# Value products of a head pair issued as one block, transposed probabilities written back into their own tiles

## The chip, the cores and the metric

The kernel runs on one core of one Trainium2 chip. The metric is the device time of one execution in microseconds (us); less is better. Five engines share the work: TensorE (PE, with its weight loads shown apart as PEld), VectorE (DVE), ScalarE (ACT), GpSimd (POOL) and SyncE (SP, which here issues the transfers). Everything is computed in 32-bit floats.

## The reference

The reference is a stack of four residual layers over 512 tokens of width 1024: a short convolution (layer A), a sparse attention with an indexer (layer B), a latent attention (layer C) and the convolution once more. The change touches B and C alone. Both end in the same attention over 16 heads of 64 value columns, swept over blocks of 128 queries:

```
logits = jnp.einsum("bqhd,bshd->bhqs", q_b, k) * scale
logits = jnp.where(mask, logits, -jnp.inf)       # key chunk <= query chunk (B: and among its top 128 keys)
p = jax.nn.softmax(logits, axis=-1)
o = jnp.einsum("bhqs,bshd->bqhd", p, v)
...
x = x + (o * jax.nn.silu(z)) @ w_out
```

In layer B `p` is taken over the selected keys only, which the kernel does with an additive mask. A query block t (0 to 3) sees t+1 key blocks of 128, so a head has 1+2+3+4 = 10 pairs of a query block and a key block.

## The kernel before, in words

Both layers call `attention(jobs, filler)` with eight jobs, one for each pair of heads. A job is cut into six chunks: for the query blocks [0, 1], then [2], then [3], one chunk for either head (e = 0, 1). A chunk passes through four steps.

- `scores(c)` (line 607) makes the logits of both heads' chunks c and c+1 on TensorE into the two PSUM banks of tag "s" (L283 in layer B, L1049 in layer C). DVE adds the mask and finds the extremum (L622) while it moves them to two SBUF tiles of tag "p"; ACT takes the exponential and the sum (L625).
- `normalise(c)` multiplies by the reciprocal of the sum (L635 on DVE), on POOL for e = 0 (L640), on ACT for e = 1 (L642).
- `turn(c)` (line 645) transposes the 128x128 blocks of the chunk on TensorE into a PSUM bank of tag "pt" (L651) and copies that bank to SBUF into a tile of tag "pt", on DVE for the last chunk of a job (L655), else on ACT (L657).
- `mix(c)` (line 660) runs behind each odd chunk: for both heads, the values of a key block (128x64) are the stationary operand and the transposed block moves past (L672). Head 0 writes partitions 0 to 63 of the bank of tag "o", head 1 partitions 64 to 127, so these matmuls use half of the array's columns each. Behind the last chunk of the job DVE takes the bank out, times the gate (L677) or as it is (L679, the last two pairs).

The profile counts two matmul instructions for one of these products: a job has 20 products and 40 instructions of line 672.

A loop over c starts `scores` four chunks ahead, then runs `normalise`, `turn(c)`, `mix(c-1)` and the filler: the projections of later groups of heads and the gates (L274 to L276, which add three matmuls each), up to a cost that is set for each chunk. Before the first chunk of a group its projections are completed.

The order on each engine is not quite that of the program. The framework simulates a timeline when the kernel is built, and issues on each engine the earliest instruction in program order whose inputs are ready in that timeline. On the chip each engine then follows the order so fixed.

Tiles come from pools by tag: 6 of tag "p", 4 of tag "pt" in SBUF, and in PSUM 2 banks of tag "pt", 1 of "o", 1 of "tr", 2 of "pj" and the two of "s". A tile can be taken when the last reader of its former content is done. After the attention, `branch_out` splits the eight gated results for the output projection (L714, L715; "po" in the profile), whose first group of columns needs the banks "pt", "pt", "o", "tr".

Of the kernel before, what the change touches and what calls it, by code (L numbers as in the profile page):

```python
# [13 lines left out]
AF = mybir.ActivationFunctionType  # L14
OP = mybir.AluOpType
AX = mybir.AxisListType

P = 128
S = 512
D = 1024  # L20
NK = D // P
NT = S // P
# [47 lines left out]
def encoder(ctx: ExitStack, tc: tile.TileContext, a, out, depth=4):  # L70
# [4 lines left out]
    act_e, dve, pool, pe = nc.scalar, nc.vector, nc.gpsimd, nc.tensor  # L75

    def const(shape, name, dtype=F32):
        return sb.tile(shape, dtype, name=name, bufs=1)


    BUFS = {"gt": 2, "rp": 5, "T": 18, "v": 4, "gate": 10, "p": 6, "pt": 4, "qk": 4, "xh": NK, "xl": NK,
            "raw": 3, "whi": 4, "wlo": 4}
    BANKS = {"pj": 2, "pt": 2, "o": 1, "tr": 1}

    def tile_of(tag, name, shape=(P, S), dtype=F32):
        return sb.tile(list(shape), dtype, name=name, tag=tag, bufs=BUFS[tag])

# [3 lines left out]
    def tiny(name, n, dtype=F32, tag="tiny"):  # L91
        return sb.tile([P, n], dtype, name=name, tag=tag, bufs=24)

    def bank(name, tag):
        return ps.tile([P, S], F32, name=name, tag=tag, bufs=BANKS[tag])

    def two_banks(name):

        b = ps.tile([P, 2, S], F32, name=name, tag="s", bufs=1)
        return [b[:, 0], b[:, 1]]  # L100
# [7 lines left out]
    clock = [0.0]  # L108
# [99 lines left out]
    o = 0  # L208
# [5 lines left out]
    o = 0  # L214
# [64 lines left out]
    def side_by_side(outs, ls, rs):  # L279

        for i, (x, y) in enumerate(((0, 0), (0, 1), (1, 0))):
            for o, l, r in zip(outs, ls, rs):
                nc.tensor.matmul(o, l[x], r[y], start=i == 0, stop=i == 2)  # L283
        clock[0] += 0.00125 * max(256, outs[0].shape[1])
# [302 lines left out]
    def attention(jobs, filler):  # L587

        early_turns[0] = False
        chunks = []
        for j in jobs:
            mine = [(j, e, ts) for ts in ([0, 1], [2], [3]) for e in range(2)]
            for i, c in enumerate(mine):
                chunks.append(c + (j["fill"][0] + (j["fill"][1] - j["fill"][0]) * (i + 1) / len(mine),))
        stage, soft, wide, outs, factors = {}, {}, {}, {}, {}

        def parts(ts):  # L600

            o = 0
            for t in ts:
                yield t, slice(o, o + (t + 1) * P)
                o += (t + 1) * P

        def scores(c):

            j, _, ts = chunks[c][:3]
            if ts[0] == 0:  # L610
                filler.through(j["after"])
            banks = two_banks("s")
            n = len(ts)
            for t, w in parts(ts):
                j["scores"]([b[:, w] for b in banks], t)
            ps_ = [tile_of("p", "p") for _ in range(2)]
            mn = [tiny("mn", n, tag="small") for _ in range(2)]
            sm = tiny("sum", 2 * n, tag="small")
            for e in range(2):
                p = ps_[e]  # L620
                for i, (t, w) in enumerate(parts(ts)):
                    dve.tensor_tensor_reduce(out=p[:, w], in0=banks[e][:, w], in1=j["masks"](t), scale=j["qs"](e, t),  # L622
                                             scalar=-GONE, op0=OP.add, op1=OP.min, accum_out=mn[e][:, i:i + 1])
                for i, (t, w) in enumerate(parts(ts)):
                    act_e.activation(p[:, w], p[:, w], AF.Exp, bias=mn[e][:, i:i + 1], scale=-1.0,  # L625
                                     accum_out=sm[:, e * n + i:e * n + i + 1])
                stage[c + e] = p, sm

        def normalise(c):

            e, ts = chunks[c][1:3]
            p, sm = stage.pop(c)
            if e == 0:
                rc = tiny("rc", 2 * len(ts), tag="small")
                dve.reciprocal(rc, sm)  # L635
                factors[c] = factors[c + 1] = rc
            rc = factors.pop(c)[:, e * len(ts):(e + 1) * len(ts)]
            for i, (t, w) in enumerate(parts(ts)):
                if e == 0:
                    pool.tensor_scalar(p[:, w], p[:, w], rc[:, i:i + 1], None, op0=OP.mult)  # L640
                else:
                    act_e.activation(p[:, w], p[:, w], AF.Copy, scale=rc[:, i:i + 1])  # L642
            soft[c] = p

        def turn(c):
            j, e, ts = chunks[c][:3]
            p = soft.pop(c)
            b = bank("pt", "pt")
            n = sum(t + 1 for t in ts) * P
            for i in range(0, n, P):  # L650
                pe.transpose(b[:, i:i + P], p[:, i:i + P], ident)  # L651
                clock[0] += 0.11
            x = tile_of("pt", "pt")
            if c % 6 == 5:
                dve.tensor_copy(x[:, :n], b[:, :n])  # L655
            else:
                act_e.activation(x[:, :n], b[:, :n], AF.Copy)  # L657
            wide[c] = x

        def mix(c):  # L660
            j, e, ts = chunks[c][:3]
            if e == 0:
                return
            if ts[0] == 0:
                outs[id(j)] = bank("o", "o")
            o = outs[id(j)]
            x = [wide.pop(c - 1), wide.pop(c)]
            for t, w in parts(ts):
                for kb in range(t + 1):
                    i = w.start + kb * P  # L670
                    for e in range(2):
                        pe.matmul(o[64 * e:64 * e + 64, t * P:(t + 1) * P], j["v"](e, kb), x[e][:, i:i + P],  # L672
                                  start=t == 0, stop=t == NT - 1 and kb == t)
                        clock[0] += 0.134
            if ts[-1] == NT - 1:
                if j["gate"]:
                    dve.tensor_tensor(j["dst"](), o, j["dst"](), op=OP.mult)  # L677
                else:
                    dve.tensor_copy(j["dst"](), o)  # L679

        N = len(chunks)
        ahead = 4
        for c in range(-ahead, N + 1):
            if c + ahead < N and c % 2 == 0:
                scores(c + ahead)
            if 0 <= c + ahead - 1 < N:
                normalise(c + ahead - 1)
            if 0 <= c < N:
                turn(c)
            if c > 0:  # L690
                mix(c - 1)
            if c + ahead < N:
                filler.to(chunks[c + ahead][3])
        while filler.step():
            pass
        early_turns[0] = True
# [23 lines left out]
    def layer_b(last):  # L720
# [42 lines left out]
        def select():  # L763
            for t in range(1, NT):
                n = (t + 1) * P
                sc = None
                for pair in range(4):
                    banks = two_banks("si")
                    ws = [slice(0, 64), slice(64, 128)]
                    side_by_side([b[:, :n] for b in banks], [[x[w, t * P:(t + 1) * P] for x in iT[pair]] for w in ws],  # L770
                                 [[x[w, :n] for x in kiT] for w in ws])
                    for e, b in enumerate(banks):
                        rel = tile_of("p", "rel")
                        act_e.activation(rel[:, :n], b[:, :n], AF.Relu)
                        w = wi[:, t, 2 * pair + e:2 * pair + e + 1]
                        if sc is None:
                            sc = tile_of("pt", "score")
                            dve.tensor_scalar(sc[:, :n], rel[:, :n], w, 0.0, op0=OP.mult, op1=OP.add)
                        else:
                            dve.scalar_tensor_tensor(sc[:, :n], rel[:, :n], w, sc[:, :n], op0=OP.mult, op1=OP.add)  # L780
                    yield
                dve.memset(sc[0:64, n - 64:n], NEG)
                for r in range(TOPK // 8):
                    m8 = tiny("m8", 8)
                    dve.max(m8, sc[:, :n])
                    dve.match_replace(out=sc[:, :n], in_to_replace=m8, in_values=sc[:, :n], imm_value=GONE)
                    if r % 2:
                        yield 0.0047 * n
                dve.tensor_scalar(mask[t], sc[:, :n], 0.5 * GONE, NEG,
                                        op0=OP.is_gt, op1=OP.mult)  # L790
# [85 lines left out]
        gate, plain = [], []  # L876
# [192 lines left out]
    for i in range(depth):  # L1069
        kind, j = i % 3, i // 3  # L1070
# [18 lines left out]
    for i in range(depth):  # L1089
        kind, j = i % 3, i // 3  # L1090
# [91 lines left out]
```

## Time and profile before

| | |
|---|---|
| median of 3 runs | 1082.23 us (1081.65 to 1082.85) |
| the profiled execution | 1082.3 us |
| its span, first to last instruction | 1080.5 us |
| mean granted TensorE clock in it | 0.999 of full speed |
| attention of layer B | from about 384 to 542 us |
| attention of layer C | from about 670 to 823 us |

The span is 1.8 us shorter than the execution's own time. A row of a timeline gives the start of a group of like instructions in us from the span's start, how long it was in work, the engine, the line, the operation, what it writes and reads, the size of the array used and of the operand, and the count; behind it, in brackets, the engine's idle time and what ended it. Matmuls overlap in the pipeline, so two that start 0.12 us apart may each be shown with 0.28 us. Prices of single matmuls are therefore taken from one start to the next.

### The profile page before, as it was taken

The page shows a single profiled execution, that of the slowest core. Times are in us where ns is not written, and L with a number is a line of the kernel's source. Part 1 is how long each engine was busy: PE and PEld are TensorE (multiplying, and loading weights), DVE is VectorE, ACT ScalarE, POOL GpSimd, SP SyncE. Part 2 cuts the span into 40 slices and gives each one's busy share as a digit, 9 for nine tenths or more (in the row PEclk, how much of TensorE's full clock was granted, in tenths as well). Part 3 has the DMA queues.
Part 4 walks back from the last instruction along what each step waited for, and adds up shares of the span by engine and source line. Part 5 has one row for each costly group of instructions (what it writes and reads, how often), then busy time and mean ns, then how long its engine had stood idle before and what let it go on. Part 6 is the DMA issues. An engine that isn't in the chain of part 4 may idle for free.

```text
span 1080.5 us, 16178 instructions
## 1 busy us (share of the span) xinstructions
PE 1061.9 (98%) x6044; PEld 881.5 (82%) x6044; DVE 520.4 (48%) x1063; ACT 514.0 (48%) x1081; POOL 693.3 (64%) x636
## 2 busy tenths in 40 slices
PE   9999999999999999999899999999989999999998
PEld 7888888898898988887688777777767888888887
DVE  7784234345588964444423244443552463344221
ACT  6343323443444466666644447875864533333331
POOL 5656555666387898586375589695934765555552
PEclk9999999999999999999999999999999999999999
DMA  6333323223222211111022221111101333332332
GB/s 225 95 101 97 98 98 98 71 78 124 72 79 78 79 60 59 59 41 59 21 86 94 63 72 50 40 42 59 60 20 59 97 96 98 96 95 89 102 101 86
DMA packets 26574, 86.43 MB, mean 80 GB/s; under 512 B 3328, under 2 KB 4224, under 8 KB 26496
## 3 DMA queue, kind: packets, MB, share of 16 engines
q1 hardware_dynamic: 26352, 85.36, 24.8%
q8 instruction: 47, 0.77, 0.3%
q14 instruction: 31, 0.25, 0.1%
q10 hardware_dynamic: 144, 0.05, 0.0%
HBM read 83.30 MB, written 2.10 MB: 79 GB/s over the span
## 4 chain that ended last, share of the span: by engine, by line
PE 91%; DVE 3%; ACT 3%; issue 1%; POOL 1%; DMA 1%; SPq 0%; DVEq 0%; POOLq 0%; ACTq 0%
PE pa L276 10%; PE pa L275 10%; PE pa L274 10%; PE po L274 5%; PE po L275 5%; PE po L276 5%; PE o L672 4%; PE pt L651 3%; PE s L1049 3%; PE pz L276 2%; PE pz L274 2%; PE pz L275 2%; PE tr L552 2%; PE s L283 2%; PE pk L274 2%; PE pq L274 2%
## 5 line engine op out<-in xcount | busy, mean ns | idle before, releaser
L155 POOL TENSOR_TENSOR wlo<-raw,whi 128x512 fp32r<-128x512 f32 (+4 forms) x315 | 402.5, 1284 | 257.5 <-ACT whi L153 250.2
L153 ACT ACTIVATE whi<-raw 128x512 fp32r<-128x512 f32 (+4 forms) x319 | 195.5, 616 | 353.1 <-PE pa L275 161.8
L275 PE MATMUL pa<-xl,whi 128*128 128x512 f32 x512 | 199.2, 389 | 0.0
L274 PE MATMUL pa<-xh,whi 128*128 128x512 f32 x512 | 199.0, 391 | 0.0
L276 PE MATMUL pa<-xh,wlo 128*128 128x512 f32 x512 | 197.4, 389 | 0.3 <-POOL wlo L155 0.3
L274 PEld LDWEIGHTS pa<-xh,whi 128*128 128x128 f32 x512 | 96.4, 188 | 20.2 <-ACT xh L346 0.3
L276 PEld LDWEIGHTS pa<-xh,wlo 128*128 128x128 f32 x512 | 96.0, 188 | 20.5 <-POOL wlo L155 0.7
L275 PEld LDWEIGHTS pa<-xl,whi 128*128 128x128 f32 x512 | 96.2, 188 | 20.2
L640 POOL TENSOR_SCALAR p<-p,rc 128x128 f32<-128x128 f32 (+1 forms) x64 | 70.3, 1105 | 55.4 <-DVE rc L635 50.1
L625 ACT ACTIVATE p<-p,mn 128x128 f32<-128x128 f32 (+3 forms) x128 | 70.9, 557 | 18.9 <-DVE mn L622 18.7
L447 DVE TENSOR_TENSOR cg<-pa,R 128x512 f32<-128x512 f32 x16 | 11.0, 690 | 129.9 <-PE pa L276 128.8
L672 PE MATMUL o<-pt,v 128*64 128x128 f32 x640 | 56.6, 283 | 1.8 <-ACT pt L657 1.4
L622 DVE CUSTOM_DVE_ANT_0 p<-s,cmask,qs 128x128 f32<-128x128 f32 (+2 forms) x80 | 37.9, 507 | 39.0 <-PE s L1049 25.6
L672 PEld LDWEIGHTS o<-pt,v 128*64 128x64 f32 x640 | 38.9, 136 | 17.9 <-issue 9.4
L651 PE MATMUL pt<-ident,p 128*128 128x128 f32 x320 | 50.8, 279 | 2.7 <-ACT pt L657 1.8
L274 PE MATMUL po<-xh,whi 128*128 128x512 f32 x128 | 50.5, 394 | 1.1 <-ACT qT L111 1.1
L274 PE MATMUL pz<-xh,whi 128*128 128x512 f32 x128 | 51.2, 400 | 0.0
L276 PE MATMUL pz<-xh,wlo 128*128 128x512 f32 x128 | 50.3, 396 | 0.4 <-POOL wlo L155 0.4
L275 PE MATMUL pz<-xl,whi 128*128 128x512 f32 x128 | 50.5, 395 | 0.0
L275 PE MATMUL po<-xl,whi 128*128 128x512 f32 x128 | 50.3, 393 | 0.0
L347 DVE SCALAR_TENSOR_TENSOR xl<-x,gains,xh 128x512 fp32r<-128x512 f32 x32 | 42.1, 1345 | 16.5 <-ACT xh L346 16.2
L275 PE MATMUL po<-glo,whi 128*128 128x512 f32 x128 | 49.8, 389 | 0.0
(243 smaller groups left out, 2444.7 us busy)
## 6 DMA issues: line engine op xcount, KB each, us to landing
raw<-in_a_in SPq DMA_DIRECT2D x63, 512.0 KB, 3.9
raw<-in_a_out SPq DMA_DIRECT2D x16, 512.0 KB, 3.9
raw<-in_b_z SPq DMA_DIRECT2D x8, 512.0 KB, 3.5
raw<-in_b_q SPq DMA_DIRECT2D x8, 512.0 KB, 3.4
raw<-in_b_k SPq DMA_DIRECT2D x8, 512.0 KB, 3.4
raw<-in_b_v SPq DMA_DIRECT2D x8, 512.0 KB, 3.7
raw<-in_b_out SPq DMA_DIRECT2D x8, 512.0 KB, 3.9
raw<-in_c_z SPq DMA_DIRECT2D x8, 512.0 KB, 3.6
```

The lines of the kernel that those rows point to most:

```text
L153: act_e.activation(hi, raw[:, j:j + m], AF.Copy)
L155: e.tensor_tensor(out=lo, in0=raw[:, j:j + m], in1=hi.bitcast(F32), op=OP.subtract)
L274: nc.tensor.matmul(o, l[0], r[0], start=first, stop=False)
L275: nc.tensor.matmul(o, l[0], r[1], start=False, stop=False)
L276: nc.tensor.matmul(o, l[1], r[0], start=False, stop=last)
L347: dve.scalar_tensor_tensor(lo, X[k], g, hi.bitcast(F32), op0=OP.mult, op1=OP.subtract)
L622: dve.tensor_tensor_reduce(out=p[:, w], in0=banks[e][:, w], in1=j["masks"](t), scale=j["qs"](e, t), scalar=-GONE, op0=OP.add, op1=OP.min, ...
L625: act_e.activation(p[:, w], p[:, w], AF.Exp, bias=mn[e][:, i:i + 1], scale=-1.0, accum_out=sm[:, e * n + i:e * n + i + 1])
L640: pool.tensor_scalar(p[:, w], p[:, w], rc[:, i:i + 1], None, op0=OP.mult)
L651: pe.transpose(b[:, i:i + P], p[:, i:i + P], ident)
L672: pe.matmul(o[64 * e:64 * e + 64, t * P:(t + 1) * P], j["v"](e, kb), x[e][:, i:i + P], start=t == 0, stop=t == NT - 1 and kb == t)
L1049: pe.matmul(o, sets[g]["q"][2 * i + e][:96, t * P:(t + 1) * P], sets[g]["k"][2 * i + e][:96, :(t + 1) * P], start=True, stop=True)
```

## The change

The products of the values no longer run behind every odd chunk but once for each pair of heads, behind its last chunk, in one go of 20 products. They begin with the newest tile: query block 3 of head 1, then head 0, and so on back to block 0. The copy of the transposed block goes back into the tile of tag "p" that it came from, the tag "pt" in SBUF is gone, and its four tiles are added to "p" (10 in place of 6). In the loop `mix(c-1)` stands ahead of `scores(c+4)` instead of behind `turn(c)`. The indexer's score tile in layer B takes a "p" tile too.

```diff
-    BUFS = {"gt": 2, "rp": 5, "T": 18, "v": 4, "gate": 10, "p": 6, "pt": 4, "qk": 4, "xh": NK, "xl": NK,
+    BUFS = {"gt": 2, "rp": 5, "T": 18, "v": 4, "gate": 10, "p": 10, "qk": 4, "xh": NK, "xl": NK,
...
         def turn(c):
...
-            x = tile_of("pt", "pt")
             if c % 6 == 5:
-                dve.tensor_copy(x[:, :n], b[:, :n])
+                dve.tensor_copy(p[:, :n], b[:, :n])
             else:
-                act_e.activation(x[:, :n], b[:, :n], AF.Copy)
-            wide[c] = x
+                act_e.activation(p[:, :n], b[:, :n], AF.Copy)
+            wide[c] = p
 
         def mix(c):
+
             j, e, ts = chunks[c][:3]
-            if e == 0:
+            if e == 0 or ts[-1] < NT - 1:
                 return
-            if ts[0] == 0:
-                outs[id(j)] = bank("o", "o")
-            o = outs[id(j)]
-            x = [wide.pop(c - 1), wide.pop(c)]
-            for t, w in parts(ts):
-                for kb in range(t + 1):
-                    i = w.start + kb * P
-                    for e in range(2):
-                        pe.matmul(o[64 * e:64 * e + 64, t * P:(t + 1) * P], j["v"](e, kb), x[e][:, i:i + P],
-                                  start=t == 0, stop=t == NT - 1 and kb == t)
-                        clock[0] += 0.134
-            if ts[-1] == NT - 1:
-                if j["gate"]:
-                    dve.tensor_tensor(j["dst"](), o, j["dst"](), op=OP.mult)
-                else:
-                    dve.tensor_copy(j["dst"](), o)
+            o = bank("o", "o")
+            first = True
+            for d in (4, 2, 0):
+                x = [wide.pop(c - 5 + d + e) for e in range(2)]
+                for t, w in reversed(list(parts(chunks[c - 5 + d][2]))):
+                    for kb in range(t + 1):
+                        i = w.start + kb * P
+                        for e in (1, 0):
+                            pe.matmul(o[64 * e:64 * e + 64, t * P:(t + 1) * P], j["v"](e, kb), x[e][:, i:i + P],
+                                      start=first, stop=t == 0)
+                            clock[0] += 0.134
+                        first = False
+            if j["gate"]:
+                dve.tensor_tensor(j["dst"](), o, j["dst"](), op=OP.mult)
+            else:
+                dve.tensor_copy(j["dst"](), o)
...
         for c in range(-ahead, N + 1):
+            if c > 0:
+                mix(c - 1)
             if c + ahead < N and c % 2 == 0:
                 scores(c + ahead)
...
             if 0 <= c < N:
                 turn(c)
-            if c > 0:
-                mix(c - 1)
...
-                            sc = tile_of("pt", "score")
+                            sc = tile_of("p", "score")
```

## Rows read from the trace of the kernel before

**Rows 1.** The page's first part: busy time in us (share of the span) and instructions of each engine over the whole span.

```profile
PE 1061.9 (98%) x6044; PEld 881.5 (82%) x6044; DVE 520.4 (48%) x1063; ACT 514.0 (48%) x1081; POOL 693.3 (64%) x636
```

**Rows 2.** The page's fourth part, the chain of work that ended last: shares of the span by engine.

```profile
PE 91%; DVE 3%; ACT 3%; issue 1%; POOL 1%; DMA 1%; SPq 0%; DVEq 0%; POOLq 0%; ACTq 0%
```

**Rows 3.** The sums by stage: for each stretch its length and the busy us (and count) of PE, PEld, DVE, ACT and POOL, then the granted clock, the DMA share and GB/s. The stretches are layer B's attention, its end, layer C's attention, its end.

```profile
384.00:520.00 136.00, 135.60 (x1129) 115.63 (x1128) 65.49 (x189) 89.43 (x221) 102.81 (x92) 1.00 0.17 55
520.00:542.00 22.00, 19.19 (x164) 14.37 (x162) 9.93 (x31) 13.73 (x36) 8.04 (x7) 1.00 0.01 2
670.00:799.00 129.00, 126.14 (x794) 96.21 (x792) 59.52 (x189) 94.75 (x245) 95.76 (x119) 1.00 0.15 46
799.00:823.00 24.00, 21.79 (x155) 15.45 (x154) 9.32 (x29) 13.21 (x35) 8.41 (x7) 1.00 0.01 1
```

**Rows 4.** The view of line 672, the value products, over the whole span: its matmuls (duration in ns least/median/most, first and last start), and what its engine sat idle for before it (us, times).

```profile
L672 PE MATMUL o<-pt,v x640: 272/273/324, 397.5 to 820.2; 128*64 128x128 f32 x160
...
  issue: 9.4, 42
  ACT pt L657: 5.0, 11
```

**Rows 5.** TensorE's timeline around a run of twelve value products that stands between projections of 256 columns.

```profile
401.70 0.28 PE L275 MATMUL pk<-wlo,xh 128*128 128x256 f32 x1
401.82 0.28 PE L276 MATMUL pk<-whi,xl 128*128 128x256 f32 x1
402.03 0.88 PE L672 MATMUL o<-pt,v 128*64 128x128 f32 x12
402.83 0.39 PE L274 MATMUL pk<-whi,xh 128*128 128x256 f32 x1
403.06 0.28 PE L275 MATMUL pk<-wlo,xh 128*128 128x256 f32 x1
```

**Rows 6.** The same timeline where a batch of twelve is cut into two and ten, then a run of sixteen between transposes, and a run of four.

```profile
397.51 0.43 PE L672 MATMUL o<-pt,v 128*64 128x128 f32 x2
397.88 0.44 PE L552 MATMUL tr<-ident,qk 128*128 128x128 f32 x2
398.25 0.87 PE L672 MATMUL o<-pt,v 128*64 128x128 f32 x10
399.05 0.39 PE L276 MATMUL pk<-whi,xl 128*128 128x256 f32 x1
...
453.11 0.55 PE L651 MATMUL pt<-ident,p 128*128 128x128 f32 x3
453.58 1.09 PE L672 MATMUL o<-pt,v 128*64 128x128 f32 x16
454.61 0.55 PE L651 MATMUL pt<-ident,p 128*128 128x128 f32 x3
454.91 0.36 PE L274 MATMUL pk<-whi,xh 128*128 128x256 f32 x1
...
738.23 0.44 PE L672 MATMUL o<-pt,v 128*64 128x128 f32 x4
```

**Rows 7.** The weight loads' timeline (PEld) around one more run of twelve, between transposes.

```profile
447.95 0.63 PEld L672 LDWEIGHTS o<-pt,v 128*64 128x64 f32 x12 [0.17 <-issue]
448.75 0.42 PEld L651 LDWEIGHTS pt<-ident,p 128*128 128x128 f32 x4 [0.17 <-issue]
```

**Rows 8.** TensorE's timeline, its rows of line 672: there are 70 of them, the first is the first of rows 6, the last stands here. Of the 70, 29 lie before 520 us, 7 in 520 to 542, 27 in 670 to 799 and 7 in 799 to 823. In the 56 of the first and third stretch, 34 have a count of 2, 6, 10 or 14 and 22 one of 4, 8, 12 or 16.

```profile
819.38 1.09 PE L672 MATMUL o<-pt,v 128*64 128x128 f32 x14
```

**Rows 9.** TensorE's timeline at the end of layer B's attention, from the scores of the last but one group (518.21) to the output projection.

```profile
518.21 0.96 PE L283 MATMUL s<-kT,qT 64*128 64x512 f32 x6
...
525.80 1.09 PE L651 MATMUL pt<-ident,p 128*128 128x128 f32 x8
...
528.42 0.97 PE L283 MATMUL s<-kT,qT 64*128 64x512 f32 x6
...
532.31 1.86 PE L672 MATMUL o<-pt,v 128*64 128x128 f32 x24
534.53 1.09 PE L651 MATMUL pt<-ident,p 128*128 128x128 f32 x8 [0.36 <-POOL p L640]
```

**Rows 10.** DVE's timeline in the same place: the copy of the last chunk of the pair before, and the first write of scores behind it.

```profile
527.38 0.68 DVE L655 COPY pt<-pt 128x512 f32<-128x512 f32 x1
529.54 0.75 DVE L622 CUSTOM_DVE_ANT_0 p<-s,mask,qs 128x512 f32<-128x512 f32 x1 [0.46 <-PE s L283]
```

**Rows 11.** TensorE's timeline in the middle of layer B's attention: the scores of query block 3 of the second pair, and the run of their value products.

```profile
410.09 0.96 PE L283 MATMUL s<-kT,qT 64*128 64x512 f32 x6
...
432.41 1.09 PE L672 MATMUL o<-pt,v 128*64 128x128 f32 x16
```

**Rows 12.** The sums of layer C's attention in stretches of 20 us, columns as in rows 3.

```profile
670.00:690.00 20.00, 19.40 (x132) 14.06 (x131) 10.08 (x37) 17.35 (x48) 19.82 (x29) 1.00 0.18 53
...
710.00:730.00 20.00, 20.00 (x117) 15.14 (x116) 9.03 (x34) 13.93 (x36) 18.53 (x28) 1.00 0.10 31
...
750.00:770.00 20.00, 20.00 (x127) 16.12 (x127) 11.35 (x43) 16.95 (x48) 18.86 (x27) 1.00 0.11 29
```

More of the change, by code (lines that the diff above doesn't have):

```diff
@@ L597, in attention @@
                 chunks.append(c + (j["fill"][0] + (j["fill"][1] - j["fill"][0]) * (i + 1) / len(mine),))
-        stage, soft, wide, outs, factors = {}, {}, {}, {}, {}
+        stage, soft, wide, factors = {}, {}, {}, {}
         def parts(ts):
@@ L645, in turn @@
         def turn(c):
-            j, e, ts = chunks[c][:3]
+            ts = chunks[c][2]
             p = soft.pop(c)
```

## The prediction, made before the changed kernel was run

> **What bounds the kernel now.** I read the page first. TensorE is busy for 1061.9 of the 1080.5 us and no other engine for more than 64% [rows 1], and the chain that ended last runs over TensorE for 91% of the span [rows 2]. So a microsecond taken from TensorE's queue is a microsecond off the time wherever TensorE has no idle time of its own. The sums by stage tell where that holds [rows 3]: in layer B's attention it idles 0.4 of 136 us, in layer C's 2.9 of 129, while at either end, where the filler has run out, it idles 2.8 of 22 and 2.2 of 24. The reader is to see a stage that is full on TensorE and, behind it, a short one that is not.
>
> But full is not the same as well used. The view of line 672 shows TensorE's weight loads idle 42 times ahead of a value product with nothing to wait for, 9.4 us in all, some 0.2 us each [rows 4]. The timeline shows why: a run of value products uses 64 of the array's columns, its neighbours use 128, and at either border the weight loads stop for 0.17 us [rows 7].
>
> **What a run costs.** Between projections of 256 columns starts are 0.12 us apart. From the last of them ahead of the run of twelve (402.03) to the second one behind it the starts go from 401.82 to 403.06, which is 1.24 us [rows 5]; two projection steps of 0.12 leave 1.00 for the twelve. What the products themselves need comes from runs of different length: 2 and 4 take 0.43 and 0.44, 10 and 12 take 0.87 and 0.88, 16 takes 1.09 [rows 5, 6]. So they go in fours (two heads, two instructions each) at 0.22 us, or 0.054 for one, and an unfinished four costs as much as a full one. Twelve are worth 0.65, and the borders of that run cost 1.00 - 0.65 = 0.35. For the run of sixteen between transposes the next start is 1.03 later (453.58 to 454.61), against 0.87 of work: 0.16 inside it, and 0.09 at its head as in rows 5 (0.21 in place of 0.12), 0.25 with nothing counted behind it [rows 6]. A run thus costs 0.25 to 0.35; I take 0.32, nearer the upper end, since behind a run the second start is late too (0.23 in place of 0.12 in rows 5), which the 0.25 leaves out.
>
> **The change, part by part.**
>
> *Runs that go away.* There are 70 runs for 16 pairs of heads, 56 of them in the two full stages [rows 8]. The full stages hold 480 of the 640 instructions, so six pairs of heads in each layer. Borders: 56 x 0.32 = 17.9 us. Of the 56, 34 end on an unfinished four, two to a broken four, 17 x 0.22 = 3.7. Together 21.6 us. The new order starts with the newest tile, so once its first product can run all the others can: a pair becomes one run of 40, no four broken. Left: 12 x 0.32 = 3.8. Saved 17.8 us.
>
> *Runs that come back.* Filler that stands earlier in the program and becomes ready in the middle of a run may still cut it, as happened at 738.23, where a run of four stands alone [rows 6]. I allow four cuts in twelve runs, each a border and a half-filled four: 4 x (0.32 + 0.11) = 1.7 us lost.
>
> *The ends.* The last pair's products of its first two chunk pairs, 24 instructions, run in the old kernel in one row at 532.31, while the last group's softmax is still to come [rows 9]. Now they stand behind the last transposes: 24 x 0.054 = 1.3, less one run saved there (0.32 + 0.22), so 0.8 us later. Behind them stands the last pair's result, but also the output projection in the two freed "pt" banks, so TensorE does not idle there. Earlier runs saved at the ends I count at nothing, since TensorE already idles among them [rows 3].
>
> *The tile that is held longer.* A "p" tile used to be free after its transposes; now it is free after the run. Ten tiles are six of this pair and four of the next, so the scores of the next pair's block 3 wait for the run: DVE's write of scores (L622) is late by the copy, 0.68 us [rows 10], plus a run of 40, 10 x 0.22 + 0.32 = 2.5: 3.2 us. Behind it on DVE stand the later score writes and the reciprocals, for which POOL, ACT and the next transposes wait. What hides it is the distance between those scores and their transposes. The shortest that the softmax takes is 528.42 to 534.53, 6.1 us [rows 9]. In the middle of a stage the distance from such scores to their value run is 22 us [rows 11], so 3.2 costs nothing there. One pair from the end it is 7.6 (518.21 to 525.80), and for the last pair there is no room [rows 9]. There the old copy began at 527.38 and the write of the last scores at 529.54, 2.2 us later [rows 10]; with 3.2 in its place the write comes 1.0 later. Bounds 0 and 3.2 for each end; I take 0.7, below that 1.0, since TensorE's queue ahead of the copy is lighter by the products that moved. Both ends with the 0.8: 2 x 1.5 = 3.0 us lost.
>
> *The copies* write as many elements from the same banks on the same engines: nothing. They can't overwrite what a transpose still reads, as each already waits for its bank. The indexer's score tile now draws on the ten tiles that its other users have too: nothing, as there are no more tiles in use than before. Ten tiles in all, as before; no transfer moves in the program.
>
> *What the other engines take back.* Filler now comes faster, and with it the conversion of weights by ACT and POOL. In layer C's attention POOL is busy for 19.8, 18.5 and 18.9 us in three stretches of 20 [rows 12]; also each run waits at its head for one last copy. Bounds: nothing, and all that those 60 of 129 us would save, half of 17.8 x 60/129 = 4.1. I take half, 2.0.
>
> **The sum:** -17.8 + 1.7 + 3.0 + 2.0 = -11.1 us. The profiled execution took 1082.3, its span 1080.5, and the median is 1082.2, so all stand for the same: 1071 us.
>
> **The rivals.**
>
> *POOL paces layer C* (0.18). For: rows 12. Against: TensorE shows no wait for POOL there, being 19.4 to 20.0 of 20 busy. If POOL sets the pace in those stretches and late copies add as much again, the loss is 4.1 to 8.2 in place of 2.0: 1073 to 1077, say 1076. [...]
>
> *The runs stay cut* (0.10): the built order breaks each pair at several places, because the copies or older filler become ready one by one. If three runs for a pair remain, 36 x 0.32 + 3.7 = 15.2 stay of 21.6 and 6.4 is saved, less 5.0 for the ends and the other engines: 1081, no change. For: the old batches were cut. Against: mostly in twos, where the second head's copy was missing, and the new order asks for that one first.
>
> *More comes out* (0.10): the 2.9 us that TensorE waits in layer C's stage [rows 3], mostly at heads of runs, go too, the ends cost nothing, nothing is taken back: 1082.3 - 17.8 - 2.9 + 1.7 = 1063.
>
> *Borders are free* (0.02): if the first weight load behind a border were hidden like any other, only the broken fours would be saved: 1082.3 - 3.7 + 5.0 = 1083.6. Against: the loads stand idle for 0.17 us at either border [rows 7]. [...]
>
> *Slower, by the held tile* (0.08): the 3.2 us are not hidden in the middle. A net gain of 11.1 is 0.7 for each of 16 pairs, so it decides where the pairs stall by more than 0.7 on average, that is, where scores lie less than 6.1 + 3.2 - 0.7 = 8.6 us ahead of their transposes in every pair. Rows 11 speak against it; near the ends it holds. If half the pairs stalled in full: 1071.2 + 8 x 3.2 - 1.4 = 1095.
>
> **How the numbers follow.** The forecast itself, 1066 to 1075, has 0.52. With the POOL case and the better one, 1063 to 1080 holds 0.80. What can be told from no change is 0.2%, 2.2 us. Faster: 0.52 + 0.18 + 0.10 = 0.80. Same: the cut runs and the free borders, 0.12 less 0.01 for their upper tail, 0.11. Slower: 0.08 and that 0.01, 0.09.
>
> **What would show it.** Right: in the new trace some 16 to 22 runs of line 672, most of x40 and about 2.4 us long; its idle time under "issue" down from 9.4 to about 3; layer B's attention shorter by 8 to 9 us, layer C's by 6 to 9, the layers A unchanged; the score writes (L622) waiting for line 672 only near the ends. Wrong: many runs of 2 to 16; L622 waiting for L672 in the middle; TensorE idle ahead of runs for L655 or L657; POOL full and TensorE waiting for "wlo".

## The result, and the profile after

The changed kernel took 1075.09 us in the median of six runs (1073.36 to 1078.64), against 1082.09 for the kernel before: a ratio of 0.9935, interval 0.9924 to 0.9946. The forecast, 1071 (1063 to 1080), holds the time; the likeliest value lies 4 us below it. The profiled execution is the slowest of the six: 1078.64 us, span 1076.9, mean granted clock 0.990. The others had 0.993 to 0.998.

In the changed kernel the transposes are line 652, their copies L655 and L657, the value products L673, their way out L678 and L680, the scores of layer C L1050.

The page's first part, busy time of each engine; it answers to [rows 1].

```profile
PE 1053.8 (98%) x6044; PEld 883.4 (82%) x6044; DVE 522.1 (48%) x1063; ACT 512.1 (48%) x1081; POOL 690.2 (64%) x636
```

TensorE's work shrank by 8.1 us with the same 6044 instructions. The view of line 673, which answers to [rows 4]: its matmuls, the idle time ahead of its weight loads, and (last line) who waited for it.

```profile
L673 PE MATMUL o<-p,v x640: 272/273/472, 409.5 to 816.5; 128*64 128x128 f32 x160
...
  issue: 6.3, 19
...
  DVE p L622: 7.7, 4
```

The timeline counts 22 runs of value products, most of 40. One from the middle of layer B, between scores:

```profile
448.23 0.96 PE L283 MATMUL s<-kT,qT 64*128 64x512 f32 x5
449.11 2.40 PE L673 MATMUL o<-p,v 128*64 128x128 f32 x40
451.45 0.50 PE L283 MATMUL s<-kT,qT 64*128 64x512 f32 x1
```

So the runs came out as foreseen. What was not foreseen stands in the sums by stage, the same stretches and columns as [rows 3]:

```profile
384.00:520.00 136.00, 133.55 (x1167) 118.34 (x1166) 70.96 (x202) 95.22 (x240) 104.21 (x93) 1.00 0.18 55
520.00:542.00 22.00, 20.52 (x148) 16.15 (x147) 6.86 (x17) 10.37 (x25) 7.60 (x7) 0.84 0.01 2
670.00:799.00 129.00, 124.00 (x810) 97.85 (x809) 63.81 (x205) 97.93 (x258) 94.48 (x115) 0.98 0.15 46
799.00:823.00 24.00, 21.64 (x142) 16.60 (x141) 5.26 (x12) 8.89 (x19) 7.34 (x6) 0.83 0.00 1
```

Behind the five busy times stands the granted clock: 1.00 in all four rows of before, now 0.84 and 0.83 at the two ends. The end of layer C in finer stretches:

```profile
790.00:793.00 3.00, 1.58 (x8) 1.12 (x8) 1.50 (x8) 2.77 (x9) 0.80 (x1) 1.00 0.00 0
793.00:801.00 8.00, 7.23 (x19) 4.48 (x19) 2.91 (x13) 5.06 (x17) 3.46 (x4) 0.57 0.00 0
801.00:807.00 6.00, 4.20 (x51) 3.11 (x49) 2.20 (x6) 3.64 (x9) 2.36 (x3) 1.00 0.00 0
807.00:814.00 7.00, 6.45 (x19) 5.19 (x20) 1.38 (x2) 0.73 (x2) 0.49 (x1) 0.51 0.00 0
```

The clock reads 1.00, 0.57, 1.00 and 0.51. TensorE is busy for only 1.58 of 3 us and 4.20 of 6, and behind each of these stretches its clock stands near 0.5: a microsecond that lies wholly in such a low stretch shows 0.50, one wholly outside it 1.00. Sums microsecond by microsecond give 13.7 us at 0.50, the half clock, here and 6.8 at the end of layer B; in the attention of the kernel before there are none. TensorE's timeline at the end of layer B:

```profile
516.29 0.95 PE L283 MATMUL s<-kT,qT 64*128 64x128 f32 x12 [0.29 <-DVE mn L622]
519.00 0.79 PE L283 MATMUL s<-kT,qT 64*128 64x384 f32 x6 [1.76 <-DVE mn L622]
519.72 1.46 PE L652 MATMUL pt<-ident,p 128*128 128x128 f32 x8
521.50 1.65 PE L283 MATMUL s<-kT,qT 64*128 64x512 f32 x6 [0.33 <-DVE mn L622]
523.09 0.91 PE L652 MATMUL pt<-ident,p 128*128 128x128 f32 x3
523.92 3.95 PE L673 MATMUL o<-p,v 128*64 128x128 f32 x40
```

The run of 40 that takes 2.40 in the middle takes 3.95 here, and six scores take 1.65 in place of 0.96 [rows 9].

### The profile page after: what moved, and what is told of

It is laid out like the page before. It is cut to its first block, busy times and chain, and to the rows that moved or that the text cites. A ratio compares the mean times of both kernels' runs of the same rounds, so it can differ in the third digit from the quotient of the medians.

```text
span 1076.9 us, 16214 instructions
## 1 busy us (share of the span) xinstructions
PE 1053.8 (98%) x6044; PEld 883.4 (82%) x6044; DVE 522.1 (48%) x1063; ACT 512.1 (48%) x1081; POOL 690.2 (64%) x636
## 4 chain that ended last, share of the span: by engine, by line
PE 90%; DVE 3%; ACT 2%; POOL 2%; issue 1%; DMA 1%; SPq 0%; DVEq 0%; ACTq 0%; POOLq 0%
PE pa L275 10%; PE pa L276 10%; PE pa L274 10%; PE po L274 6%; PE po L276 5%; PE po L275 5%; PE o L673 3%; PE pt L652 3%; PE s L1050 3%; PE pz L276 2%; PE pz L274 2%; PE pz L275 2%; PE s L283 2%; PE tr L552 2%; PE pq L274 2%; PE pk L275 1%
## 5 line engine op out<-in xcount | busy, mean ns | idle before, releaser
L622 DVE CUSTOM_DVE_ANT_0 p<-s,cmask,qs 128x128 f32<-128x128 f32 (+2 forms) x80 | 37.9, 506 | 32.0 <-PE s L1050 19.7
L652 PEld LDWEIGHTS pt<-ident,p 128*128 128x128 f32 x320 | 38.7, 147 | 16.0 <-issue 7.7
L657 ACT ACTIVATE p<-pt 128x384 f32<-128x384 f32 (+1 forms) x80 | 39.1, 508 | 22.8 <-PE pt L652 22.7
L269 POOL TENSOR_TENSOR y<-mean,minus_half 128x16 f32<-128x16 f32 (+1 forms) x18 | 49.4, 2746 | 0.6
```

The costliest lines, as they stand in the source:

```text
L269: pool.tensor_tensor(out=y, in0=m, in1=minus_half[:, :n], op=OP.pow)
L657: act_e.activation(p[:, :n], b[:, :n], AF.Copy)
```

## The experiments

In the table "layer B" and "layer C" is the time in the profiled execution from the first start of the layer's scores to the start of its last value product, "low" the time therein at the half clock, by sums for each microsecond. Without an interval a time is a single run (that of "before" is a median of six); the layers' times are always those of one profile.

| kernel | us | ratio to before, interval | layer B (low) | layer C (low) |
|---|---|---|---|---|
| before | 1082.1 | | 168.35 (0) | 159.62 (0) |
| changed, first profile | 1075.1 | 0.9935, 0.9924 to 0.9946 | 164.07 (6.8) | 159.22 (13.7) |
| changed, second profile | 1072.5 | | 162.14 (0) | 156.42 (6.8) |
| before, heads swapped | 1071.9 | 0.9905, 0.9891 to 0.9918 | 164.08 (0) | 153.49 (0) |
| changed, last two pairs in batches | 1068.0 | 0.9866, 0.9853 to 0.9879 | 162.23 (3.4) | 151.59 (0) |
| changed, tiles freed | 1069.2 | 0.988, 0.9865 to 0.9895 | 161.74 (3.4) | 153.16 (3.4) |
| changed, idle matmuls added | 1075.8 | 0.9942, 0.9929 to 0.9954 | 165.89 (0) | 155.71 (0) |
| changed, only last pair but one in batches | 1073.8 | 0.9917, 0.9905 to 0.993 | 164.22 (6.8) | 155.42 (6.8) |
| changed, only last pair in batches | 1072.0 | 0.9909, 0.9894 to 0.9925 | 162.93 (3.4) | 154.34 (3.4) |
| changed, last three pairs in batches | 1068.7 | 0.9876, 0.9863 to 0.989 | 163.05 (3.4) | 152.24 (0) |
| changed, oldest first | 1075.7 | 0.9939, 0.9926 to 0.9951 | 163.58 (0) | 158.03 (0) |
| batches and tiles freed | 1066.9 | 0.9857, 0.984 to 0.9873 | 161.06 (0) | 151.64 (0) |
| changed, heads apart | 1077.5 | | 165.61 (0) | 156.84 (0) |
| changed, heads apart, again | 1079.2 | | 166.40 (3.4) | 156.83 (0) |

**The price of borders and fours.** The kernel before, with the heads of each product pair swapped, so that a batch asks for the later copy first:

```diff
-                    for e in range(2):
+                    for e in (1, 0):
```

> The kernel before with one line changed: inside each batch of value products head 1, whose copy comes last, goes first. If runs and broken fours are priced as in the prediction (0.32 us a run, 0.22 a broken four), the order built has 52 runs instead of 70 and nearly no broken four: 18 x 0.32 + 19 x 0.22 = 10 us less, 1072 us, with the clock as before (0.999), since the ends keep their products. If instead the gain of the change comes from moving and gathering the products, this is worth 3 us at most: 1079 to 1081.

1071.92 us (1071.6 to 1072.77), as expected. In the view of line 672, what the loads sat idle for, and two runs of the timeline:

```profile
  ACT pt L657: 6.5, 9
  issue: 5.6, 24
```

```profile
397.26 0.44 PE L672 MATMUL o<-pt,v 128*64 128x128 f32 x4
398.00 0.66 PE L672 MATMUL o<-pt,v 128*64 128x128 f32 x8
```

The 2 and 10 of [rows 6] are a 4 and an 8 here: where a batch is still cut, it is mostly between fours. There are 52 runs, not 70, and the borders idle 24 times, not 42. One line gives 10.2 us, more than the whole change in its median. The prices of the forecast hold together; this run does not tell them apart. No time in either attention is at the half clock.

**The last two pairs in batches.** The changed kernel, but the last two pairs of each layer mixed behind each pair of chunks as before:

```diff
+            late = c >= len(chunks) - 12
-            if e == 0 or ts[-1] < NT - 1:
+            if e == 0 or (ts[-1] < NT - 1 and not late):
                 return
...
-            for d in (4, 2, 0):
+            for d in ((4,) if late else (4, 2, 0)):
```

> The changed kernel, but in the last two pairs of heads of each layer the value products run behind each pair of chunks again (newest tile first). If the loss is at the two ends alone, where the products no longer fill TensorE's waits, the full stages keep their 13 us and the ends are as before: 1067 to 1070 us, clock 0.998 or more, and the spread of the runs small again. If the missing gain lies in the full stages or the clock falls for another reason, it stays at 1074 to 1076.

1068.01 us (1066.94 to 1068.46), as expected, better than both kernels. DVE's score writes (L622) now wait 2.0 us for value products, not 7.7. Of the changed kernel's four waits those at the ends are gone (2.76 us at 525.9, 2.93 at 802.6); the two that are left, 2.0 us, lie in layer C's full stage (at 681 and 764 here). So what is missing from the forecast's gain is at the ends. But this edit changes three things at once: the filling of TensorE's waits, the held tiles and the clock. The next runs take them apart.

**The held tiles alone.** The copies of the first four chunks of the last pair but one go to tiles of tag "qk"; the single run of 40 stays:

```diff
+            x = tile_of("qk", "late") if len(chunks) - 12 <= c < len(chunks) - 8 else p
```

> The changed kernel, but four chunks of the last pair but one have their transposed blocks copied to spare tiles (tag qk, idle by then), so the last scores find free tiles and needn't wait for that pair's run. If the held tile is what costs at the ends, the two waits of L622 for the value run (2.8 and 2.9 us) go and the time falls by 4 to 6 us: 1069 to 1071. If it is the missing fill and the clock, the waits go too, but the time falls by no more than 2 us: 1073 to 1075, and the clock still drops at the ends.

1069.16 us (1068.87 to 1070.13). The idle time of DVE ahead of L622:

```profile
  PE o L674: 2.0, 2
```

The wait falls to 2.0, as with the batches, and 5.9 of their 7.1 us are there, though no short run has come back. That is the held tile's side, but the time at the half clock fell as well, from 20.5 us to 6.8.

**The clock alone.** Two matmuls that nobody reads behind each copy of the last twelve chunks of a layer except the very last, to keep TensorE busy; the product itself is whole:

```diff
+            if len(chunks) - 12 <= c < len(chunks) - 1:
...
+                for _ in range(2):
+                    pe.matmul(held["keep"][:, :P], ones, p[:, :P], start=True, stop=True)
```

> The changed kernel with two matmuls that nobody reads (ones times a copied tile, 128x128, about 0.21 us each) behind the copy of each of the last eleven chunks but one, so 22 for each layer, 4.7 us of added work a layer. If TensorE's falling clock at the ends is a cost of its own, the granted clock stays at 0.998 or more and the runs spread no wider than before; the time is 1072 or less plus what of the 9.4 us isn't placed in idle time, so 1070 to 1077. If the clock is only a sign of the waits and costs nothing, the time rises by the added work that isn't hidden: 1077 to 1082.

1075.81 us (1075.39 to 1077.23), no time at the half clock. The added work as the timeline shows it:

```profile
526.53 0.77 PE L652 MATMUL pt<-ident,p 128*128 128x128 f32 x5
527.61 0.71 PE L663 MATMUL keep<-p,ones 128*128 128x128 f32 x4 [0.31 <-ACT p L657]
528.15 0.49 PE L652 MATMUL pt<-ident,p 128*128 128x128 f32 x3
```

Layer B, 165.89, is 3.75 us longer than in the changed kernel's second profile (162.14), both at the full clock: by the medians, 1075.8 and 1075.1, the added instructions (44 in a layer) cost about what the clock gives back. The time lies in the range of the theory that the clock costs, but only 1.2 us below that of the other; alone it settles nothing.

**Either pair alone.** The condition `late` of the batches, for one pair at a time:

```diff
-            late = c >= len(chunks) - 12
+            late = len(chunks) - 12 <= c < len(chunks) - 6
```

> The changed kernel with the last pair but one alone cut into three batches again, the last pair in one run. That frees its tiles early for the last scores and fills the waits ahead of its own end. If the end is lost to the held tile and to the idle time and falling clock just ahead of it, this brings nearly all that splitting both pairs brought: 1068 to 1070 us. If it is lost to the products that stand behind the last transposes, it stays near 1073 to 1075.

1073.81 us (1070.66 to 1075.26): the time of the second theory. What the score writes (L622) wait for value products:

```profile
  PE o L676: 2.0, 2
```

The sums at its two ends, and TensorE's waits in the first of them:

```profile
525.00:533.00 8.00, 6.09 (x21) 4.75 (x19) 0.86 (x2) 2.23 (x6) 1.56 (x1) 0.57 0.00 0
802.00:809.00 7.00, 6.18 (x18) 5.02 (x19) 1.39 (x2) 1.23 (x3) 0.76 (x1) 0.51 0.00 1
...
524.36 0.88 PE L652 MATMUL pt<-ident,p 128*128 128x128 f32 x6 [1.69 <-POOL p L640]
527.14 1.97 PE L652 MATMUL pt<-ident,p 128*128 128x128 f32 x8 [1.91 <-POOL p L640]
```

The 2.0 us are again those in layer C's stage. So no score waits for a held tile at the ends, and still 6.8 us at either end are at the half clock, among waits in which the last pair's batches stand when both pairs are cut. The missing short runs are enough for that, without the held tile.

With the last pair (`late = c >= len(chunks) - 6`):

> The changed kernel with the very last pair alone cut into three batches, the last but one in one run. The last scores still wait for the held tiles. If the held tile and the idle time ahead of the last pair but one's run are the cause, little comes back: 1073 to 1075 us, clock still below 0.998. If it is the last pair's products, 1068 to 1070.

1072.03 us (1071.28 to 1073.44), between the two cases. Each of the two kernels has time at the half clock at both ends, 13.7 and 6.8 us in all. Neither pair alone is the cause, and the spread of the first, 4.6 us for one program, pointed to the clock. With the last three pairs in batches nothing more comes:

> The last three pairs of either layer in batches. The wait of L622 for the value run, 1.2 us where the last pair but two still ran in one go, goes; against it stand two more runs in either layer, 4 x 0.32 = 1.3 us. 1067 to 1069: no clear difference to the version with two pairs (1068.0).

1068.69 us (1067.88 to 1070.35), not to be told from two pairs.

**The order within a pair.** The changed kernel with the oldest tile and head 0 first:

```diff
-            for d in (4, 2, 0):
+            for d in (0, 2, 4):
...
-                        for e in (1, 0):
+                        for e in (0, 1):
```

> The changed kernel with the products of a pair in the old order, block 0 of head 0 first. The order built has them in more than 50 runs again, half of them with a broken four. If the gain of the full stages hangs on the newest tile going first, it is gone (the prediction's price of a run gives 1082), and the loss at the ends stays: 1080 to 1087 us. If gathering the products behind the last chunk is enough by itself, it stays at 1073 to 1077.

1075.67 us (1075.36 to 1076.08): missed by 4 us, and in the range for "gathering is enough", though the trace shows that it is not. Some pairs of layer C, in TensorE's timeline:

```profile
729.18 0.43 PE L673 MATMUL o<-p,v 128*64 128x128 f32 x2
...
730.81 0.44 PE L673 MATMUL o<-p,v 128*64 128x128 f32 x4
...
731.85 0.65 PE L673 MATMUL o<-p,v 128*64 128x128 f32 x6
...
735.32 1.09 PE L673 MATMUL o<-p,v 128*64 128x128 f32 x14
```

There are 57 runs, not 70: three pairs of layer B stay whole. At the ends the products stand between the waits again, and no time is at the half clock. So the order is what makes runs of 40, and it costs as well: whole runs leave the ends empty. The median equals the changed kernel's, with more runs and a better clock; against what the changed kernel shows at the full clock (162.14 in layer B, some 153.6 in layer C as worked out below) this order is some 6 us slower.

**Batches and freed tiles together.**

> The version with the last two pairs of each layer in batches (1068.0 us), and besides it the copies of the first four chunks of the last pair but one go to tiles of their own, so that the last scores wait for no value run. In the version with batches DVE's score writes still waited 2.0 us for value products. If the held tile costs anything there, those 2.0 us or a part of them come out: 1066 to 1067.5. If the waits for the tiles matter only where TensorE has nothing else to run, which the batches now give it, nothing comes out: 1067.5 to 1069. The version with the tiles freed and no batches took 1069.2.

1066.85 us (1066.28 to 1067.51). By the time alone the held tile would still count, though the two versions' times overlap. The profile says otherwise: L622 waits 2.0 us as without the freeing, since those waits lie in layer C's stage, which the tiles of the last pair but one can't touch; layer C takes 151.64 for 151.59, and layer B is shorter by 1.17 where it has no time at the half clock and the other had 3.4. Freeing adds nothing to the batches that these profiles show.

**The heads apart, twice, and the same program twice.** First all blocks of head 1 of a query block, then all of head 0, in the same run of 40:

```diff
-                    for kb in range(t + 1):
-                        i = w.start + kb * P
-                        for e in (1, 0):
+                    for e in (1, 0):
+                        for kb in range(t + 1):
+                            i = w.start + kb * P
```

> The changed kernel with the two heads of a tile one behind the other: all blocks of head 1, then all of head 0, in place of the heads in turn; the same 40 instructions in the same run. The forecast's price is 0.22 us for a four, two instructions of either head, and the same for an unfinished one. If the halves of a four must stand next to each other, a run of 40 holds 14 steps of 0.22 where a product pairs up only at a change of head, or 20 where none does: 3.1 or 4.4 us in place of 2.2, so 0.9 or 2.2 us more for each of 16 pairs, 1089 or 1110 us. If an instruction costs 0.054 wherever it stands, nothing changes: 1073 to 1079.

1077.53 us, in the range for "nothing changes", and yet the run is longer, 2.89 for 2.40:

```profile
449.80 2.89 PE L673 MATMUL o<-p,v 128*64 128x128 f32 x40
452.62 0.50 PE L283 MATMUL s<-kT,qT 64*128 64x512 f32 x1
```

That is 16 x 0.49 = 7.8 us more work at 2.4 us more time than the changed kernel's median. This profile has no time at the half clock. So both kernels went once more:

> The changed kernel once more, nothing edited, for a second profile of the same program. [...] If the loss is in the order of the instructions and their waits, the ends take 28.3 us (layer B) and 33.0 us (layer C) again, whatever the clock.

> The kernel with the two heads of a tile one behind the other once more: it took 1077.5 us at a clock of 1.000, with each run of 40 products 0.49 us longer, 2.89 for 2.40. [...] If the clock matters little, it takes 1077 to 1078 again, whatever the clock.

The changed kernel took 1072.49, 6.15 less than in its first profile. At the end of layer B, as above:

```profile
514.91 0.95 PE L283 MATMUL s<-kT,qT 64*128 64x128 f32 x12 [0.29 <-DVE mn L622]
517.62 0.79 PE L283 MATMUL s<-kT,qT 64*128 64x384 f32 x6 [1.76 <-DVE mn L622]
518.35 1.09 PE L652 MATMUL pt<-ident,p 128*128 128x128 f32 x8
520.12 0.96 PE L283 MATMUL s<-kT,qT 64*128 64x512 f32 x6 [0.68 <-DVE mn L622]
521.07 0.52 PE L652 MATMUL pt<-ident,p 128*128 128x128 f32 x3
521.52 2.40 PE L673 MATMUL o<-p,v 128*64 128x128 f32 x40
...
526.41 1.78 PE L652 MATMUL pt<-ident,p 128*128 128x128 f32 x11 [1.68 <-ACT p L657]
```

The same rows with the same waits of 0.29 and 1.76 us ahead of them, and then 1.09, 0.96 and 2.40 where there were 1.46, 1.65 and 3.95. Only the clock, and what it stretches, differs. Layer B is 1.93 us shorter without its 6.8 us at the half clock, layer C 2.80 shorter with 6.8 in place of 13.7; 1.38 of the 6.15 lie ahead of layer B, where nothing was changed and where the start of its scores comes at 371.1 to 373.2 us from profile to profile. The heads apart repeat it: layer C is 156.84 and 156.83 with no time at the half clock in either, layer B 165.61 and 166.40 with 0 and 3.4. The line through the fastest and the slowest of the first six runs, 1073.36 at 0.998 and 1078.64 at 0.990, is 6.6 us for 0.01; it gives some 1074.7 at a clock of 0.996 and lies 2.2 too high there: of the 6.15 us the 1.38 ahead of layer B have nothing to do with the clock.

## Why the prediction was right, and where its sum was not

**The borders and fours were sized right.** 0.32 for a border and 0.22 for a four together gave 1072 for the swapped heads, and 1071.9 was measured. 22 runs lie in the forecast's 16 to 22; 18 of them are in the full stages, so there are six cuts for the four allowed (two pairs came in three parts, of 20, 4 and 16).

**At the full clock the sum holds, with errors in its parts.** Layer B gains 168.35 - 162.14 = 6.2 us. For layer C the full clock has to be worked out: 156.42 less another 2.8 is 153.6; the heads apart, 156.84 less 8 x 0.49, give 152.9; so some 6.0 to 6.7. Together some 12.5, against 11.1 in the forecast: some 1070 us. By layer the forecast's terms come to 6.9 and 4.2 (its 29 and 27 runs at their prices, half the cuts and half the ends for either, the other engines' 2.0 all in C). So in layer C the 2.0 for the other engines do not seem to have been taken back. The version with the last two pairs in batches agrees: with no time at the half clock its layer C is 8.0 us shorter than before, and the forecast without the 2.0 and without its half of the ends is 4.2 + 2.0 + 1.5 = 7.7. Nothing shows POOL pacing layer C. The sign by layer was missed for layer B, where 8 to 9 us were to come and 4.3 did, 6.2 at the full clock; in layer C, of 6 to 9, it was 0.4, and only the worked-out 6.0 to 6.7 lie in the range.

**The failed step is "The ends".** It says "Earlier runs saved at the ends I count at nothing, since TensorE already idles among them". They cost time. Those short runs stood in TensorE's waits for the softmax; without them it idles longer (0.29, 1.76, 0.68 and 1.68 us at the end of layer B in the second profile, 4.4 in all, against 2.8 before [rows 3]), and behind such waits its granted clock fell to 0.50, in the first profile at both layers' ends, in the second at layer C's: the mean was 0.990 to 0.998 in all seven executions, against 0.999 before. In the first profile this takes 1.9 us in layer B and some 6 in layer C, on scores, transposes, products and the first steps of the output projection. At the six runs' usual clock, 0.994, it is about two thirds of that, some 5 us by this estimate: the difference between 1070 and 1075. The forecast's rows had a clock of 1.00 throughout [rows 3], and no term asked what keeps it there. The 1.4 us more at the full clock and the 5 lost stand against each other: that the time came out within 4 us is in part luck. The time at the half clock differs between the two profiles of this one program: 20.5 and 6.8 us.

**The held tile was undersized.** The forecast took 0.7 us for each end (bounds 0 and 3.2). L622 waits 2.8 and 2.9 us at the two ends in the first profile, 0.9 and 2.6 in the second. The other two of its four waits, 2.0 us together, lie in layer C's stage, where the forecast expected none; no run shows whether they cost time. With the tiles freed, and 0.3 to 0.4 us taken off for each microsecond at the half clock, the two layers come to 160.6 and 151.9, against 162.1 and some 153: about 1.3 for each end. That is the wait alone; in time, with what it adds at the half clock, freeing the tiles gave 5.9 us (1075.1 to 1069.2) and the batches on top 2.3 (to 1066.9). The shares depend on the order, since the batches free the tiles as well: alone they gave 7.1. No run holds the tiles with the short runs in place, so whether the held tile by itself brings the clock down is not shown; that the missing short runs do is (13.7 us at the half clock with the last pair but one in batches).

**One sign misread.** "Issue" idle time of the value products went from 9.4 to 6.3, not to 3: a border that is left shows 0.33 in place of 0.22. The mean of 42 had cheaper ones in it: 30 of them were 0.16 to 0.18 us, of the 19 only 5. The runs' own length, 2.40 of which 2.13 lie between the first and last start, bears the price out all the same.

**What stays open.** Batches, swapped heads, oldest first: each keeps the clock up at one end or both. That filled waits do it fits all of them, but what exactly lets the clock fall does not show: with equal waits it fell in one execution and not in the other.

## What to carry to other kernels

Where the filler runs out, small pieces of work that stand in an engine's waits are worth more than their own length: join them where the stage is full, and leave them apart at its ends, which here took 1075.1 to 1068.0 us. Ask there too what a longer block keeps occupied: freeing its tiles alone took it to 1069.2. Before restructuring, try the one-line order that asks for the latest input first; it gave 10.2 of the 15 us. And where two profiles of one program differ, compare the granted clock by stretch before explaining the difference by the program.

## What the runs showed of the hardware

**The clock can fall behind short waits.** In the changed kernel's first profile the single idle times ahead of the low stretch that begins at 520 us are 0.29 and 1.76 us, and TensorE had worked between them. A microsecond at the half clock cost 0.28 us in layer B (1.93 for 6.8) and 0.41 in layer C (2.80 for 6.8), less than the 0.5 that a queue without waits would lose by it, the author's estimate from the granted 0.50.

**Two halves need not alternate.** With the heads apart a run of 40 took 2.89 us, in the alternating order 2.40. In the run that starts at 812.80 TensorE has 16 instructions in work in the microsecond from 813 on and 23 in the next; in the alternating order it has 24 in one that lies wholly in a run of 40 (from 522 on in the changed kernel's second profile). So the run begins more slowly and then comes near the other's pace, and 0.49 us is lost, not 0.9 or 2.2. Why the pace changes the rows don't show, as they don't name the head.
